# A weight subtraction on GpSimd issued as four instructions of 256 columns in place of one of 1024

## The chip, the cores and the metric

The kernel runs on one core of a Trainium2 chip. A core has five engines with an instruction queue each: TensorE (PE, with its weight loads shown apart as PEld), VectorE (DVE), ScalarE (ACT), GpSimd (POOL) and SyncE (SP, which here issues the DMAs). Engines wait for each other by semaphores. The metric is device microseconds of one execution; lower is better. The kernel before takes 1645.46 us, the median of three runs from 1644.57 to 1647.92.

## The reference

One step of a small diffusion backbone on 128 context tokens and 512 latent tokens, 1024 wide, in float32. There are two layers: layer 0 mixes tokens by a bidirectional gated linear recurrence, layer 1 by a convolution of width 31; each is followed by a squared-ReLU MLP four times as wide. Each sub-layer has this form:

```
hp = rmsnorm(xp, norm_mlp[i]) * (1.0 + m_ctx[4]) + m_ctx[3]
hs = rmsnorm(xs, norm_mlp[i]) * (1.0 + m_lat[4]) + m_lat[3]
xp = xp + m_ctx[5] * sqrelu_mlp(hp, mlp_w1[i], mlp_w2[i])
xs = xs + m_lat[5] * sqrelu_mlp(hs, mlp_w1[i], mlp_w2[i])
```

The scales, shifts and gates come from a matrix product of the conditioning vector (the modulation). Nearly all of the work is in dense products: the mixers' projections and the MLPs.

## The kernel before

Activations are kept with the model's width on the 128 partitions and the 640 tokens on the columns, in two token halves (320 and 320, later 304 and 336). A dense product is cut into units: one unit makes 128 outputs of one token half out of 1024 inputs, in eight steps k of 128 inputs.

To keep float32 accuracy, each factor is split into a high part, which the fast matmul format represents, and a low part, the rest. A step is then three matmuls: high weights by high activations (L178), low weights by high activations (L181), high weights by low activations (L182). A unit has 24.

The weights of a unit come by one DMA of 128 x 1024 into `rw` (4 buffers). ACT casts them to `wh` (L161, 5 buffers), and then POOL or DVE subtracts: `wl = rw - wh` (L163, 5 buffers). Which of the two does it is fixed by the unit's place in the list of weights (L162): POOL takes units 0 and 2, the 32 of the output projection (listed once per token half) and of layer 0's first MLP quarter, every second one of the next 48, and then 144 in a row up to the middle of layer 1's MLP; DVE takes the others, most of the first 40 and the last 70 among them. POOL does 202, DVE 132. The function `fetch` (L154) is called so that the weights of a unit are requested three units ahead of its matmuls.

DVE and ACT also do what follows a product: `hr` and the splits `ch`/`cl`, `dh`/`dl` of the MLP's hidden activations (L167, L168, L701, L702), the residual additions `xr` (L285), the squares and sums of a norm (`nsq` on ACT L254, `nacc` on DVE L255), the normed and modulated values `nt` (L276, L268) with their splits, the taps of the convolution `ps_cv` (L792) with its layer norm (`lsum` L804, `yc` L820), and the dot products of the modulation (`scratch`, L128). Such steps are put between the units by a budget per unit (`between`, L193). A scheduler beneath writes each engine's queue in the order in which the program issues, with waits where a tile is read or overwritten.

Of the kernel before, what the change touches and what calls it, by code (L numbers as in the profile page):

```python
# [9 lines left out]
F32 = mybir.dt.float32  # L10
# [3 lines left out]
ALU = mybir.AluOpType  # L14
# [3 lines left out]
D = 1024  # L18
KT = D // P
# [50 lines left out]
def hybrid_step(ctx: ExitStack, tc: tile.TileContext, xt, vec, pos, masks, ident_in, state, c_rows, w_mod0, w_modt,  # L70
# [23 lines left out]
    def v(name):  # L94
        return vt[:, VEC[name]]

# [1 line left out]
    mod = const.tile([P, 2, 48, 2], F32, name="mod")  # L98
    amod = const.tile([P, 2, 2, KT, 2], F32, name="amod")

    def mod_done(layer, j, src):
        """Adds the bias to chunks 2j and 2j+1, and for a chunk that scales makes norm_w * (1 + scale)."""
        bm = ap(vt, VEC["b_mod"].start + layer * 48 + j * 16, [[4, 4], [1, 4], [0, 2]])
        dst = ap(mod, (layer * 48 + j * 16) * 2, [[8, 4], [2, 4], [1, 2]])
        dve.tensor_tensor(dst, src, bm, ALU.add)
        for which in range(2):
            if j != (0, 2)[which]:
                continue
            base = (layer * 48 + (8, 32)[which]) * 2
            nw = VEC[("norm_mix", "norm_mlp")[which]].start + layer * 8  # L110
            dve.scalar_tensor_tensor(
                amod[:, layer, which].rearrange("p k s -> p (k s)"), ap(mod, base, [[1, 16]]), 1.0,
                ap(vt, nw, [[1, 8], [0, 2]]), ALU.add, ALU.mult)

    def mod_steps(cbs, raw_m, scratch, layer, j0, wm):
        """Chunks from 2 * j0 on of a layer's modulation, as dot products along rows of the transposed weights."""
        for s in range(2):
            cr = raw.tile([P, D], F32, tag="rw", name="cr")
            sync.dma_start(cr[:], c_rows[s:s + 1].partition_broadcast(P))
            act.activation(cbs[:, s], cr[:], AF.Sigmoid)  # L120
            dve.tensor_tensor(cbs[:, s], cbs[:, s], cr[:], ALU.mult)
        box = {}

        def step(i, s):
            if s == 0:
                box["w"] = wm()
                sync.dma_start(box["w"][:], w_modt[layer * 32 + i - 16 * (1 - layer)])
            tc.keep_in_program_order(dve.scalar_tensor_tensor(  # L128
                scratch, box["w"][:], 1.0, cbs[:, s], ALU.mult, ALU.mult, accum_out=raw_m[:, i, s:s + 1]))
            if s == 1 and i % 16 == 15:  # L130
                mod_done(layer, i // 16, ap(raw_m, (i - 15) * 2, [[8, 4], [2, 4], [1, 2]]))

        return [lambda i=i, q=q: step(i, q) for i in range(16 * j0, 48) for q in range(2)]
# [1 line left out]
    def mvec(layer, chunk, m, s):  # L135
        return mod[:, layer, chunk * 8 + m, s:s + 1]

# [1 line left out]
    MLP = [[[w_mlp[l, c, u] for u in range(16)] for c in range(4)] for l in range(2)]  # L139
    PW1 = [w_pw1[u] for u in range(16)]  # L140
    PW2 = [w_pw2[u] for u in range(8)]
# [12 lines left out]
    def fetch(upto):  # L154
        while len(split_w) < min(upto, len(plan)):
            i = len(split_w)
            rw = raw.tile([P, KT, P], F32, tag="rw", name="rw")
            sync.dma_start(rw[:], plan[i])
            wh = wpool.tile([P, KT, P], F32R, tag="wh", name="wh")
            wl = wpool.tile([P, KT, P], F32R, tag="wl", name="wl")  # L160
            act.copy(wh[:], rw[:])  # L161
            eng = pool if i in (0, 2) or 40 <= i < both_n or busy <= i < calm or (both_n <= i < busy and i % 2) else dve  # L162
            eng.tensor_tensor(wl[:], rw[:], wh[:].bitcast(F32), ALU.subtract)  # L163
            split_w.append((wh, wl))

    def split(src, hi, lo, eng=dve):
# [39 lines left out]
            bg.pop(0)[1]()  # L206

    def linear(n, acts, evac, cols, group=8, after=between, u0=0, done=None):
        """n units of weights against the token halves given in cols: {half: (lo, hi)}."""
        first = pos_w[0]  # L210
        pos_w[0] += n
        for g0 in range(0, n, group):
            us = range(g0, min(g0 + group, n))
            for half in cols:
                lo, hi = cols[half]
                for u in us:
                    fetch(first + u + 3)
                    evac(u0 + u, half, lo, hi, half_unit(split_w[first + u], acts[half], hi - lo))
                    after()
                if done and g0 + group >= n:  # L220
                    done(half)

# [1 line left out]
    def inv_rms(tp, acc, n, by_token):  # L224
        """1/rms of the columns of acc, the squares summed along D but for the partitions, on all partitions."""
        ps = axp.tile([P, 512], F32, tag="ax", name="ps_n")
        if not by_token:
            pe.matmul(ps[:, :n], ones[:], acc, start=True, stop=True)
# [10 lines left out]
        for i in range(4):  # L239
            pe.matmul(ps[:, i * c:(i + 1) * c], rc[:c, i:i + 1].broadcast_to([c, P]), ident[:c, :c],  # L240
                      start=True, stop=True)
        return ps[:, :n]

    def rms_stat(tp, xs, n, by_token=False):
        """Steps that leave 1/rms over the KT tiles xs(k) in the returned box."""
        box = {}

        def sq(k):
# [49 lines left out]

    both = {0: COLS[0][0], 1: COLS[0][1]}

# [1 line left out]
    h = {0: new_act("a"), 1: new_act("b")}  # L302
    first_ps = [[(mmp, "mm"), (scp, "sc")][half][0].tile([P, 512], F32, tag=("mm", "sc")[half], name=f"ps_f{half}")
                for half in (0, 1) for _ in range(3)]
    with tc.tile_pool(name="start", bufs=1) as st:
# [24 lines left out]
                act.activation(t[:], x0[:, k], AF.Square)  # L330
                dve.tensor_tensor(acc[k // 4][:], acc[k // 4][:], t[:], ALU.add)

        # shift and scale in blocks of columns, so that the first products start with the first block
        wmb = {}

        def first_load(m0, m1):
# [79 lines left out]
                {"L": first_load, "M": first_mods, "N": first_norm, "P": first_vecs}[a[0]](*BLOCKS[i])  # L416
        pos_w[0] = 3
        sync.dma_start(vt[:, n0:], vec[:, n0:])
        # forget gate lower bounds: softmax over the layer axis, cumulated, less the first row
        lbt = const.tile([P, 16], F32, name="lbt")  # L420
        lbe = const.tile([P, 16], F32, name="lbe")
        lbr = const.tile([P, 16], F32, name="lbr")
# [38 lines left out]
    with tc.tile_pool(name="wm0", bufs=1) as wmp, tc.tile_pool(name="hd", bufs=1) as hd:  # L461
# [31 lines left out]
            return evac  # L493

        def blocks(x, y, evac, w=SB, other=False):
            """Scores within blocks of w tokens (or across two neighbours), source token on the partition."""
            ps = scp.tile([P, 512], F32, tag="sc", name="ps_sc")
            for t in range(NTILE):
                for r in range(0, P, w):
# [4 lines left out]
            evac(ps[:, :NTILE * w].rearrange("p (t c) -> p t c", c=w))  # L504

        def decay(hs, li):
            """Keeps the operands of a level aside and takes the running products one level up."""
            lv = LEVELS[li]
            a = hs.a
            nb = NT // (2 * lv)  # L510
# [30 lines left out]
            decay(hs, 0)  # L541

        def score(hs, li):
            """li < 0: equal tokens; else the pairs that part at that level."""
            if li < 0:
                hs.sc = hd.tile([P, NTILE, SB], F32, tag="scs", name="scs")
                blocks(hs.ks[:], hs.q[:], lambda ps: act.copy(hs.sc[:], ps))
# [105 lines left out]
        while todo or mods:  # L653
            (todo or mods).pop(0)()

# [1 line left out]
    xpool = ctx.enter_context(tc.tile_pool(name="xpool", bufs=1))  # L657
    xr = xpool.tile([P, KT, NT], F32, name="xr")
    tp = ctx.enter_context(tc.tile_pool(name="tp", bufs=1))
# [33 lines left out]
    oright.close()  # L693
    rp = ctx.enter_context(tc.tile_pool(name="rp", bufs=2))

# [1 line left out]
    def hid_evac(hid):  # L697
        def evac(u, half, lo, hi, ps):
            n = hi - lo
# [15 lines left out]
        linear(8, hid, residual(xr, layer, 5), cols, group, done=done)  # L715

    def start_norm(layer, which, half, cols, first=True, by_token=False, on_dve=ND):
        """Queues a norm of one token half; returns its last step."""
        h[half] = new_act("ab"[half])
        steps = norm_steps(tp, xr, layer, which, h[half], *cols, by_token, on_dve)  # L720
        bg[:] = steps + bg if first else bg + steps
# [3 lines left out]
    A1, B1 = ({0: COLS[1][0]}, {1: COLS[1][1]})  # L725
    both1 = {0: COLS[1][0], 1: COLS[1][1]}

    # w_out, then the first MLP; the first token half runs ahead of the second
    budget[1] = 3.0
    for cols in (A0, B0):  # L730
        linear(8, on, residual(xr, 0, 2), cols, done=lambda half: start_norm(0, 1, half, COLS[0][half], False, TM0, ND0))
# [235 lines left out]
```

## Time and profile before

| what | before |
|---|---|
| timed runs | 1644.57, 1645.46, 1647.92 us |
| profiled execution: span, first to last instruction | 1641.7 us |
| PE busy | 1586.2 us, 97% |
| DVE busy | 1315.9 us, 80% |
| ACT busy | 765.8 us, 47% |
| POOL busy | 530.0 us, 32% |
| POOL's 202 subtractions wl | 504.2 us, 2502 ns each |
| mean granted clock of TensorE | 0.984 |

The page gives the profiled execution's span and no time of its own around it. Busy time is the union of an engine's instructions; a wait is idle time of an engine right before an instruction, put down to what ended it. The span is one execution with profiling, the timed runs are others without.

### The profile page before, as it was taken

Reading aid. Unit: us, or ns where it says so; the run is one execution under the profiler, and the core shown is the slowest. Engines: PE = TensorE matmul, PEld = TensorE weight load, DVE = VectorE, ACT = ScalarE, POOL = GpSimd, SP = SyncE. Lnnn points to the kernel's source line nnn. Section 1 sums busy time; section 2 is a strip of 40 time slices with the busy share of each in tenths; the row PEclk is TensorE's granted clock in tenths of the full one; section 3 lists DMA queues with packets and bytes.
Section 4 is the critical chain, followed back from the end, with each engine's and each line's share of the span. In section 5 each row is a group of like instructions: output and inputs, shape, how many; then the busy total and the mean of one; then the engine's idle time right before and its main releaser. Section 6 shows DMA issues by size and latency. Waiting matters only on the chain.

```text
span 1641.7 us, 31432 instructions
## 1 busy us (share of the span) xinstructions
PE 1586.2 (97%) x12810; PEld 1542.8 (94%) x12810; DVE 1315.9 (80%) x2222; ACT 765.8 (47%) x1227; POOL 530.0 (32%) x257
## 2 busy tenths in 40 slices
PE   8999999999998999999999999999999899999997
PEld 7899999988898999999999999989999899999997
DVE  5788888878778998888989998999999767555544
ACT  3666655566355314334443435664344545334331
POOL 3100000002363423333666665567776520000000
PEclk8999999999998999999999999999999999999999
DMA  9333333334243566676444443334444344444411
GB/s 364 117 111 118 116 110 113 120 95 158 99 148 107 173 205 219 220 227 207 155 130 153 144 152 130 124 126 162 154 154 155 100 158 154 142 141 142 142 39 65
DMA packets 71296, 240.06 MB, mean 146 GB/s; under 512 B 7792, under 2 KB 14576, under 8 KB 70128
## 3 DMA queue, kind: packets, MB, share of 16 engines
q1 hardware_dynamic: 71152, 238.06, 43.7%
q8 instruction: 101, 1.65, 0.4%
q14 instruction: 43, 0.35, 0.1%
HBM read 234.36 MB, written 3.67 MB: 145 GB/s over the span
## 4 chain that ended last, share of the span: by engine, by line
PE 61%; DVE 29%; ACT 4%; issue 3%; POOL 2%; DMA 1%; SPq 0%; DVEq 0%; ACTq 0%; POOLq 0%
PE ps_mm L178 18%; PE ps_mm L182 18%; PE ps_mm L181 18%; DVE ps_cv L792 6%; DVE cl L168 3%; DVE scratch L128 3%; DVE nacc L255 2%; POOL wl L163 2%; DVE hr L702 2%; PE ps_sc L502 2%; DVE dl L168 1%; DVE wl L163 1%; DVE nt L276 1%; DVE nt L268 1%; ACT wh L161 1%
## 5 line engine op out<-in xcount | busy, mean ns | idle before, releaser
L163 POOL TENSOR_TENSOR wl<-rw,wh 128x1024 fp32r<-128x1024 f32 x202 | 504.2, 2502 | 754.7 <-ACT wh L161 705.2
L161 ACT CAST wh<-rw 128x1024 fp32r<-128x1024 f32 x334 | 348.4, 1046 | 314.5 <-PE ps_mm L182 220.8
L178 PE MATMUL ps_mm<-bh,wh 128*128 128x320 f32 (+1 forms) x1000 | 317.7, 318 | 2.9 <-DVE ub L770 1.6
L178 PE MATMUL ps_mm<-ah,wh 128*128 128x320 f32 (+1 forms) x1000 | 314.8, 315 | 4.6 <-DVE hr L702 2.7
L182 PE MATMUL ps_mm<-al,wh 128*128 128x320 f32 (+1 forms) x1000 | 310.8, 311 | 2.6 <-DVE al L168 2.6
L181 PE MATMUL ps_mm<-bh,wl 128*128 128x320 f32 (+1 forms) x1000 | 311.2, 311 | 0.0
L181 PE MATMUL ps_mm<-ah,wl 128*128 128x320 f32 (+1 forms) x1000 | 311.1, 311 | 0.0
L182 PE MATMUL ps_mm<-bl,wh 128*128 128x320 f32 (+1 forms) x1000 | 310.8, 311 | 0.0
L792 DVE SCALAR_TENSOR_TENSOR ps_cv<-ub,vt,ps_cv 128x319 f32<-128x319 f32 (+1 forms) x464 | 228.5, 553 | 0.4
L178 PEld LDWEIGHTS ps_mm<-ah,wh 128*128 128x128 f32 x1000 | 191.4, 191 | 9.8 <-issue 3.1
L182 PEld LDWEIGHTS ps_mm<-al,wh 128*128 128x128 f32 x1000 | 191.2, 191 | 4.0 <-DVE al L168 3.1
L181 PEld LDWEIGHTS ps_mm<-ah,wl 128*128 128x128 f32 x1000 | 191.4, 191 | 3.2 <-issue 2.6
L178 PEld LDWEIGHTS ps_mm<-bh,wh 128*128 128x128 f32 x1000 | 188.0, 188 | 5.8 <-DVE ub L770 1.9
L163 DVE TENSOR_TENSOR wl<-rw,wh 128x1024 fp32r<-128x1024 f32 x132 | 162.5, 1232 | 38.7 <-ACT wh L161 38.7
L181 PEld LDWEIGHTS ps_mm<-bh,wl 128*128 128x128 f32 x1000 | 187.9, 188 | 0.5
L182 PEld LDWEIGHTS ps_mm<-bl,wh 128*128 128x128 f32 x1000 | 188.1, 188 | 0.1
L182 PE MATMUL ps_mm<-dl,wh 128*128 128x320 f32 (+1 forms) x576 | 180.7, 314 | 2.4 <-DVE dl L168 2.4
L182 PE MATMUL ps_mm<-cl,wh 128*128 128x320 f32 (+1 forms) x576 | 177.5, 308 | 5.0 <-DVE cl L168 5.0
L178 PE MATMUL ps_mm<-dh,wh 128*128 128x320 f32 (+1 forms) x576 | 181.6, 315 | 0.0
L181 PE MATMUL ps_mm<-dh,wl 128*128 128x320 f32 (+1 forms) x576 | 180.2, 313 | 0.0
L178 PE MATMUL ps_mm<-ch,wh 128*128 128x320 f32 (+1 forms) x576 | 177.9, 309 | 0.4 <-ACT ch L167 0.4
L285 DVE SCALAR_TENSOR_TENSOR xr<-ps_mm,mod,xr 128x128 f32<-128x128 f32 (+2 forms) x240 | 97.4, 432 | 99.8 <-PE ps_mm L182 99.8
(209 smaller groups left out, 2625.4 us busy)
## 6 DMA issues: line engine op xcount, KB each, us to landing
rw<-in_w_mlp SPq DMA_DIRECT2D x230, 512.0 KB, 3.3
wm<-in_w_modt SPq DMA_DIRECT2D x80, 512.0 KB, 4.1
rw<-in_w_pw SPq DMA_DIRECT2D x48, 512.0 KB, 3.3
rw<-in_w_in SPq DMA_DIRECT2D x40, 512.0 KB, 3.5
wmb<-in_w_mod SPq DMA_DIRECT2D x8, 1024.0 KB, 10.1
rw<-in_w_out SPq DMA_DIRECT2D x16, 512.0 KB, 3.4
x<-in_xt SPq DMA_DIRECT2D x8, 320.0 KB, 5.5
xr<-in_xt SPq DMA_DIRECT2D x8, 320.0 KB, 5.8
```

Of the source, the lines that this page charges most:

```text
L128: tc.keep_in_program_order(dve.scalar_tensor_tensor(scratch, box["w"][:], 1.0, cbs[:, s], ALU.mult, ALU.mult, accum_out=raw_m[:, i, s:s + 1]))
L161: act.copy(wh[:], rw[:])
L163: eng.tensor_tensor(wl[:], rw[:], wh[:].bitcast(F32), ALU.subtract)
L168: eng.tensor_tensor(lo, src, hi.bitcast(F32), ALU.subtract)
L178: first = pe.matmul(ps[:, :n], wh[:, k, :], hi[:, :n], start=k == 0, stop=False)
L181: pe.matmul(ps[:, :n], wl[:, k, :], hi[:, :n], start=False, stop=False)
L182: pe.matmul(ps[:, :n], wh[:, k, :], lo[:, :n], start=False, stop=k == KT - 1)
L255: dve.tensor_tensor(box["acc"][:, :n], box["acc"][:, :n], t[:, :n], ALU.add)
L285: dve.scalar_tensor_tensor(x[:, u, a:b], ps[:, a - lo:b - lo], mvec(layer, chunk, u, s), x[:, u, a:b], ALU.mult, ALU.add)
L502: pe.matmul(ps[r:r + w, t * w:(t + 1) * w], x[:, s0:s0 + w], y[:, t0:t0 + w], start=True, stop=True, tile_position=(0, r))
L702: dve.tensor_tensor(r[:, :n], ps, r[:, :n], ALU.mult)
L792: dve.scalar_tensor_tensor(box[i][:, :m], u[:, j:j + m], w, box[i][:, :m], ALU.mult, ALU.add)
```

## The change

The subtraction of L163 is put into a loop. On POOL it is issued four times, each over two of the eight steps k, that is 256 of 1024 columns; on DVE the loop has one turn and the instruction is as before. Comments are taken out, which moves line numbers (the subtraction is L165 after, the matmuls L180, L183 and L184).

```diff
             eng = pool if i in (0, 2) or 40 <= i < both_n or ... else dve
-            eng.tensor_tensor(wl[:], rw[:], wh[:].bitcast(F32), ALU.subtract)
+            step = KT // 4 if eng is pool else KT
+            for k in range(0, KT, step):
+                eng.tensor_tensor(wl[:, k:k + step], rw[:, k:k + step], wh[:, k:k + step].bitcast(F32), ALU.subtract)
             split_w.append((wh, wl))
```

POOL's queue from the start to the first MLP, before (`x` counts equal instructions in a row; `bl` are low activations, `xr` the residual stream):

```order
L163 TENSOR_TENSOR wl<-rw,wh 128x1024 x2
L168 TENSOR_TENSOR bl<-x_129,bh 128x320 x4
L433 CAST mask<-mf 128x160
L168 TENSOR_TENSOR bl<-x_129,bh 128x320 x4
L441 MEMSET sel 128x64
L442 MEMSET sel 128x1
L163 TENSOR_TENSOR wl<-rw,wh 128x1024
L297 TENSOR_TENSOR xr<-xr,pe_t 128x512 x8
L163 TENSOR_TENSOR wl<-rw,wh 128x1024 x59
```

And the same piece of POOL's queue after:

```order
L165 TENSOR_TENSOR wl<-rw,wh 128x256 x8
L170 TENSOR_TENSOR bl<-x_129,bh 128x320 x4
L435 CAST mask<-mf 128x160
L170 TENSOR_TENSOR bl<-x_129,bh 128x320 x4
L443 MEMSET sel 128x64
L444 MEMSET sel 128x1
L165 TENSOR_TENSOR wl<-rw,wh 128x256 x4
L299 TENSOR_TENSOR xr<-xr,pe_t 128x512 x8
L165 TENSOR_TENSOR wl<-rw,wh 128x256 x236
```

Each subtraction has become four in its own place, and nothing else has moved. PE's queue at the start of the first unit of the output projection (`ch`, `cl` are activations), with the semaphores that each matmul waits for, before:

```order
L181 MATMUL ps_mm<-ch,wl 128x320 [waits Pool_49]
L182 MATMUL ps_mm<-cl,wh 128x320
L178 MATMUL ps_mm<-ch,wh 128x320 [waits Activation_49]
L181 MATMUL ps_mm<-ch,wl 128x320
L182 MATMUL ps_mm<-cl,wh 128x320
L178 MATMUL ps_mm<-ch,wh 128x320 [waits Activation_49]
L181 MATMUL ps_mm<-ch,wl 128x320
L182 MATMUL ps_mm<-cl,wh 128x320
```

And after:

```order
L183 MATMUL ps_mm<-ch,wl 128x320 [waits Pool_49]
L184 MATMUL ps_mm<-cl,wh 128x320
L180 MATMUL ps_mm<-ch,wh 128x320 [waits Activation_49]
L183 MATMUL ps_mm<-ch,wl 128x320
L184 MATMUL ps_mm<-cl,wh 128x320
L180 MATMUL ps_mm<-ch,wh 128x320 [waits Activation_49]
L183 MATMUL ps_mm<-ch,wl 128x320 [waits Pool_49]
L184 MATMUL ps_mm<-cl,wh 128x320
```

PE's order is the same; the matmul with low weights waits for POOL once in two steps k instead of once a unit. The orders on DVE, ACT and SP are the same before and after.

## Rows read from the trace of the kernel before

**Rows 1.** The page's busy time of each engine: us, share of span, instructions.

```profile
PE 1586.2 (97%) x12810; PEld 1542.8 (94%) x12810; DVE 1315.9 (80%) x2222; ACT 765.8 (47%) x1227; POOL 530.0 (32%) x257
```

**Rows 2.** Windows: stretch, length, busy us (instructions) by engine, clock, DMA.

```profile
480.00:1340.00 860.00, 823.22 (x5536) 814.79 (x5535) 771.90 (x1332) 383.64 (x600) 463.82 (x209) 0.98 0.49 160
780.00:830.00 50.00, 45.49 (x294) 44.50 (x293) 47.47 (x67) 24.13 (x43) 28.74 (x27) 0.97 0.44 148
1110.00:1290.00 180.00, 170.97 (x1189) 168.80 (x1188) 174.01 (x347) 79.02 (x115) 122.90 (x52) 0.98 0.45 150
```

**Rows 3.** Waits of PE, 480 to 1340: us in total, times, longest us.

```profile
PE ps_n L228 <- DVE nacc L255: 8.8, 4, 3.2
PE ps_n L236 <- DVE nacc L255: 7.6, 1, 7.6
```

**Rows 4.** Costliest groups: busy us, mean ns | idle us ahead, what ended most.

```profile
L163 POOL TENSOR_TENSOR wl<-rw,wh 128x1024 fp32r<-128x1024 f32 x202 | 504.2, 2502 | 754.7 <-ACT wh L161 705.2
...
L181 PE MATMUL ps_mm<-ah,wl 128*128 128x320 f32 (+1 forms) x1000 | 311.1, 311 | 0.0
```

**Rows 5.** Instructions of nacc and scratch on DVE: ns min/median/max, first and last start.

```profile
L255 DVE TENSOR_TENSOR nacc<-nacc,nsq x70: 444/502/2679, 448.5 to 1631.9; 128x320 f32<-128x320 f32 x28, 128x304 f32<-128x304 f32 x21, 128x336 f32<-128x336 f32 x21
...
L128 DVE SCALAR_TENSOR_TENSOR scratch<-wm,cbs x96: 1206/1215/3299, 515.1 to 799.0; 128x1024 f32<-128x1024 f32 x96
```

**Rows 6.** Timeline of POOL and DVE near 1043: start us, length us, instruction.

```profile
1042.81 2.40 POOL L163 TENSOR_TENSOR wl<-rw,wh 128x1024 fp32r<-128x1024 f32 x1 [8.54 <-ACT wh L161]
...
1045.17 2.65 POOL L163 TENSOR_TENSOR wl<-rw,wh 128x1024 fp32r<-128x1024 f32 x1
...
1043.14 2.42 DVE L255 TENSOR_TENSOR nacc<-nacc,nsq 128x320 f32<-128x320 f32 x1 [0.34 <-ACT nsq L254]
...
1043.14 7.59 DVE L255 TENSOR_TENSOR nacc<-nacc,nsq 128x320 f32<-128x320 f32 x3 [0.34 <-ACT nsq L254]
```

**Rows 7.** Timeline of POOL and DVE near 58, two POOL subtractions of 320 columns.

```profile
57.91 0.88 POOL L168 TENSOR_TENSOR bl<-x,bh 128x320 fp32r<-128x320 f32 x1 [5.72 <-ACT bh L167]
...
58.74 1.12 POOL L168 TENSOR_TENSOR bl<-x,bh 128x320 fp32r<-128x320 f32 x1
...
58.17 0.96 DVE L168 TENSOR_TENSOR al<-x,ah 128x320 fp32r<-128x320 f32 x1
```

**Rows 8.** Timeline of POOL, six subtractions in a row from 1111.

```profile
1111.02 14.22 POOL L163 TENSOR_TENSOR wl<-rw,wh 128x1024 fp32r<-128x1024 f32 x6 [5.18 <-ACT wh L161]
```

**Rows 9.** Timeline of DVE ahead of PE's five largest stalls: the long instructions.

```profile
502.18 2.62 DVE L255 TENSOR_TENSOR nacc<-nacc,nsq 128x320 f32<-128x320 f32 x1
...
505.80 1.56 DVE L255 TENSOR_TENSOR nacc<-nacc,nsq 128x320 f32<-128x320 f32 x1 [0.54 <-ACT nsq L254]
...
540.12 3.02 DVE L128 SCALAR_TENSOR_TENSOR scratch<-wm,cbs 128x1024 f32<-128x1024 f32 x1
...
543.07 2.65 DVE L168 TENSOR_TENSOR dl<-hr,dh 128x320 fp32r<-128x320 f32 x1
...
819.25 2.26 DVE L268 TENSOR_SCALAR nt<-nt,amod,mod 128x128 f32<-128x128 f32 x1
...
823.73 2.63 DVE L276 TENSOR_TENSOR nt<-xr,rs 128x320 f32<-128x320 f32 x1
...
1266.05 2.05 DVE L804 TENSOR_TENSOR lsum<-lsum,yc 128x336 f32<-128x336 f32 x1
...
1271.86 3.54 DVE L820 TENSOR_TENSOR yc<-yc,mu 128x336 f32<-128x336 f32 x3
...
1277.76 2.84 DVE L255 TENSOR_TENSOR nacc<-nacc,nsq 128x336 f32<-128x336 f32 x2
...
1283.44 3.00 DVE L255 TENSOR_TENSOR nacc<-nacc,nsq 128x336 f32<-128x336 f32 x2 [0.28 <-ACT nsq L254]
```

**Rows 10.** Windows behind two of the stalls; the last but two column is the clock.

```profile
507.40:512.50 5.10, 5.09 (x23) 5.09 (x24) 0.65 (x2) 0.70 (x2) 0.00 (x0) 0.50 0.30 103
...
547.30:553.40 6.10, 6.08 (x23) 6.08 (x24) 5.13 (x10) 2.04 (x5) 0.00 (x0) 0.50 0.45 163
```

## The prediction

> **What bounds the kernel now.** I read the busy shares first: TensorE (PE) is busy 97% of 1641.7 us [rows 1], so only three things can move the time: PE's idle time, a lower clock, or new PE work. POOL, the engine that is edited, is busy 32%. Next the windows: of 860 us between 480 and 1340, where nearly all of POOL's subtractions run, PE is busy 823.2, so it idles 36.8 us [rows 2]; that is what a change on POOL can give back or add to. The waits name who ends that idle time: VectorE (DVE), above all its sums of squares, 7.6 us in one wait and 8.8 in four [rows 3]. No row of PE's waits there names POOL, and the groups of instructions agree: PE's products with the low weights (L181) have idle time 0.0, while POOL stands idle 754.7 us ahead of its 202 subtractions, 705.2 of it for ScalarE's casts [rows 4]. The low halves are early; making their first quarter earlier still is worth nothing to PE.
>
> So why would POOL matter? Look at one and the same DVE instruction: the sum nacc takes 0.444 us at least, 0.502 in the median, 2.679 at most, and scratch 1.206, 1.215 and 3.299 [rows 5]. The stretch of nacc around 1043 us shows why. POOL runs 1042.81 to 1045.21; nacc starts at 1043.14 and ends at 1045.56, 0.35 us after POOL did, three times in a row, 7.59 us for three [rows 6]. An addition with both operands in SBUF is held until the subtraction that runs on POOL is over. The reader is to see a second thing in these rows: POOL's second subtraction starts at 1045.17, queued right behind the first, and yet nacc gets in between them; the subtraction takes 2.65 instead of 2.40. A waiting DVE instruction gets through after one POOL instruction, and costs POOL 0.25.
>
> **The change part by part.** Removed: 202 POOL subtractions of 1024 columns. Added: 808 of 256 columns. Everything else stands in the same order on every engine; PE gets three more waits on POOL for each of 202 units.
>
> Price of a piece. Two POOL subtractions of 320 columns stand back to back, the second starting 58.74 - 57.91 = 0.83 us after the first [rows 7]; six of 1024 columns take 14.22 us, 2.37 each [rows 8]. The line through both is 0.13 + 0.00219 per column: 0.69 for 256 columns, 2.76 for four, 0.39 more per unit, 79 us over 202. Bounds: a piece can't be under a quarter of 2.37 (0.59, if nothing is fixed) nor over the 0.83 that 320 columns took; four cost 2.37 to 3.32. I take 0.69, nearest to the 320 columns in size. The cover is POOL's idle time, and what is queued behind POOL's pieces are its own next pieces and a few memsets. Between 1110 and 1290 POOL is busy 122.9 of 180 us in 52 instructions [rows 2]; with 0.39 on each that is 143, still inside. Cover gone is a rival below.
>
> The Perfetto Trace Analysis page of the Trainium skill (section GPSIMD Engine Instruction) advises to time POOL by start-to-start spacing, not by reported durations. By durations (0.88 for 320 columns, 2.40 for 1024 [rows 6, 7]) the line would give 0.74 a piece and 2.96 for four; the sum below would lose another 2 us.
>
> Added waits on PE: 606 more, each on a piece that is long done. L181's idle time of 0.0 with 202 such waits today [rows 4] prices them at 0; if one cost the 0.02 us of a semaphore instruction that I allow as the upper end, 606 cost 12.
>
> Shorter holds on DVE. A DVE instruction that arrives at random in a POOL instruction waits half of it: 1.18 us now, 0.35 with pieces. POOL is running 2.76/2.37 = 1.17 times as long, so 0.35 of the waiting stays and 0.65 goes. Rows 7 show the pattern at nearly the new size: the DVE subtraction al, caught in a 320-column POOL piece, took 0.96, not 2.4, and the next piece 1.12 instead of 0.88. I count the DVE rows ahead of PE's five largest stalls [rows 9], with 0.5 as the free length (rows 5) of an instruction of about 320 columns, and 1.21 for scratch:
> - 500 to 507: two nacc, 2.62 and 1.56, so 3.2 held; 0.65 of it 2.1. The wait is 7.6 [rows 3], so much of it stays.
> - 540 to 547: scratch 3.02 and dl 2.65, 4.0 held, 2.6 back.
> - 818 to 827: nt 2.26 and nt 2.63, 3.9 held, 2.5 back.
> - 1043 to 1050: three nacc in 7.59, 6.1 held, 4.0 back, but the wait is only 3.2 [rows 3]: 3.2.
> - 1266 to 1287: lsum 2.05, three yc in 3.54, two nacc in 2.84, two in 3.00: 1.5 + 2.0 + 1.8 + 2.0 = 7.4 held, 4.8 back.
>
> Together 15.2. The five places can't take more than 7.6 + 4.0 + 3.9 + 3.2 + 7.4 = 26 of the 36.8 us; the other 10.5 lie in short waits where one DVE instruction in between is late, of which I take 4. What is late next: the casts on ScalarE between two DVE steps of a norm, and PE itself.
>
> Room for both. Between 780 and 830 DVE is busy 47.5 of 50 us and POOL 28.7 [rows 2]: there the two already exclude each other most of the time, and POOL's extra time must come from somewhere. 27 POOL instructions less 16 memsets are 11 subtractions, 11 x 0.39 = 4.3 us; I charge all of it.
>
> Clock. Right after a long stall the granted clock is 0.50, its lower level of 1.2 GHz: 23 matmuls in 5.1 us after 507, 23 in 6.1 after 547 [rows 10], against 860/5536 = 0.155 each over the stretch with its stalls: 1.5 and 2.5 us lost. The stall at 544 should all but vanish and take its stretch along, that of 507 shrink; with the shorter ones behind other stalls I take 3.
>
> Sum: 15.2 + 4 - 4.3 + 3 = 17.9 us less. The profiled execution's span goes from 1641.7 to 1623.8. The three timed runs lie 2.9 to 6.2 us above that span, the median 3.8, time around the span that the edit doesn't touch; 1645.5 - 18 = 1627.5.
>
> **The rivals.**
> - POOL falls behind (slower). Place: 800 to 1330, where every unit's low half is POOL's and PE takes 24 matmuls of 171/1189 = 0.144, 3.45 us, a unit. A piece at its upper bound, 0.83, makes 3.32; with one DVE instruction let in, 0.25, 3.57 a unit. From 0.80 a piece on, POOL is the slower one and the spare buffers only delay it. Some 150 units (530 us by 3.45) late by 0.12 each are 18 us; DVE, held by a POOL that never rests, gets back only half of the forecast's gain, 9: 18 - 9, 9 us slower, 1654. For it: each piece offers another place for a DVE instruction to push in. Against: the 0.83 was measured for 320 columns, a fourth more.
> - POOL's four queued pieces don't let DVE in between. Then a hold is 2.76 instead of 2.37, the waits of 36.8 us grow by 0.17: 6 us slower, 1651.5. The GPSIMD Engine Reference of the Trainium skill (section Instruction dispatch) speaks for it: each of POOL's eight cores starts the next instruction as soon as its own share of the last is done, without waiting for the others, so there need be no moment at which all have let go. Against: in rows 6 and 7 the second POOL instruction was queued and ready, and DVE got in each time.
> - No change: DVE's holds shrink but PE's stalls are ended by something beside them (the casts, the order of the queue), as most of the 7.6 us are: 15.2 + 4 falls to a quarter, 5, less 4.3: 1645.
> - More than forecast: all holds at the five places (22, by each wait's limit) and half of the 10.5 vanish and the clock never falls there (6): 33 us, 1612.
> - PE's added waits are not free: 12 us of them eat most of the gain: 1639.5.
>
> **How the numbers follow.** A difference below 0.2%, 3.3 us, can't be told from none here. Forecast (10 to 26 us less) 0.52; more 0.12; added waits or a half-behind POOL (4 to 10 less) 0.12; no change 0.08; POOL behind 0.10; DVE not let in 0.06. Faster 0.76, same 0.08, slower 0.16. The likeliest case's own range is 1619.5 to 1635.5; for 8 in 10, with the bounds 0.59 and 0.83, I go from 1612 to 1650.
>
> **What would show it.** POOL: 808 subtractions, start to start near 0.69, busy time near 580 to 620 us. The longest nacc, cl and dl near 1.2 instead of 2.6; scratch near 2 instead of 3.3. PE's waits for DVE between 480 and 1340 near 20 us, the stall at 544 gone, that at 500 still there. L181 still without idle time. I am wrong if nacc still takes 2.4 us beside POOL (not let in), if PE waits for wl (POOL behind), or if DVE's holds shrink and PE's stalls stay (no change).

## The result, and the profile after

The changed kernel takes 1619.37 us (median of four runs, 1616.84 to 1620.54), beside it the kernel before 1646.66 (four runs): ratio 0.9837, 95% interval 0.9823 to 0.9851. That is 27.3 us less; 1627.5, 18 less, was forecast.

The profiled execution's span falls from 1641.7 to 1614.9 us. The page of the changed kernel, its busy times as in [rows 1]:

```profile
PE 1578.3 (98%) x12810; PEld 1536.0 (95%) x12810; DVE 1249.4 (77%) x2222; ACT 761.9 (47%) x1227; POOL 694.0 (43%) x863
```

The 26.8 us split in two. Span less PE's busy time is PE's idle time: 55.5 before, 36.6 after, 18.9 less. The other 7.9 are PE's busy time itself, for the same 12810 matmuls: the mean granted clock is 0.989 instead of 0.984. A second profile of the changed kernel (below) splits its gain into 16.6 and 7.4. DVE, whose instructions are the same 2222, is busy 66.5 us less. The time in which it was held counted as its busy time.

The windows of the changed kernel, to be laid beside [rows 2]; the second row is the stretch between the two matmuls that the kernel before starts at 780 and 830 us, so it holds the same work as the second row there. The first columns are length, PE, PEld, DVE, ACT and POOL, the last but two the granted clock:

```profile
480.00:1320.00 840.00, 821.40 (x5609) 815.02 (x5608) 725.85 (x1341) 384.92 (x611) 617.64 (x767) 1.00 0.50 166
773.04:820.96 47.92, 45.17 (x294) 44.22 (x293) 40.25 (x67) 24.30 (x43) 41.34 (x61) 0.96 0.47 154
```

PE's idle time in the stretch of POOL's work goes from 36.8 to 18.6 us. The second row is the place with "no room for both": POOL is now busy 41.3 us instead of 28.7, and still DVE needs only 40.3 us, instead of 47.5, for the same 67 instructions, and the stretch is 2.1 us shorter.

PE's waits in the changed kernel between 470 and 1320 (in total, times, longest, in us), where [rows 3] were:

```profile
PE ps_n L230 <- DVE nacc L257: 2.8, 2, 1.7
PE ps_n L238 <- DVE nacc L257: 2.6, 1, 2.6
PE ps_mm L180 <- ACT nt L268: 2.6, 1, 2.6
PE ps_mm L180 <- ACT ch L169: 2.3, 1, 2.3
PE ps_mm L180 <- DVE xr L287: 2.1, 2, 1.3
PE ps_mm L184 <- DVE cl L170: 1.8, 5, 0.9
```

The 7.6 for nacc has become 2.6 and the 8.8 has become 2.8; waits for ScalarE, the next in the chain, have moved up. The groups that answer to [rows 4], from the page:

```profile
L165 POOL TENSOR_TENSOR wl<-rw,wh 128x256 fp32r<-128x256 f32 x808 | 668.8, 861 | 568.1 <-ACT wh L161 561.6
...
L183 PE MATMUL ps_mm<-ah,wl 128*128 128x320 f32 (+1 forms) x1000 | 308.0, 308 | 0.0
```

The added waits of PE cost nothing: 0.0 again. Last the tiles that DVE makes, as in [rows 5] (ns, minimum, median, maximum):

```profile
L257 DVE TENSOR_TENSOR nacc<-nacc,nsq x70: 444/527/7968, 451.3 to 1604.2; 128x320 f32<-128x320 f32 x28, 128x304 f32<-128x304 f32 x21, 128x336 f32<-128x336 f32 x21
L128 DVE SCALAR_TENSOR_TENSOR scratch<-wm,cbs x96: 1208/1236/1768, 512.0 to 789.6; 128x1024 f32<-128x1024 f32 x96
L170 DVE TENSOR_TENSOR dl<-hr,dh x64: 493/502/1043, 529.4 to 1548.9; 128x320 fp32r<-128x320 f32 x32, 128x336 fp32r<-128x336 f32 x32
```

The holds are as long as a piece now: dl 1.04, scratch 1.77. One row doesn't fit: a nacc of 7.97 us. The timeline near 1040, on POOL and then on DVE, shows the common case (start and length in us, xN equal instructions in a row):

```profile
1039.58 5.28 POOL L165 TENSOR_TENSOR wl<-rw,wh 128x256 fp32r<-128x256 f32 x6
...
1041.52 1.02 DVE L257 TENSOR_TENSOR nacc<-nacc,nsq 128x304 f32<-128x304 f32 x1
1042.46 0.86 DVE L270 TENSOR_SCALAR nt<-nt,amod,mod 128x320 f32<-128x320 f32 x1
1043.24 1.01 DVE L257 TENSOR_TENSOR nacc<-nacc,nsq 128x304 f32<-128x304 f32 x1
```

Six pieces take 5.28, 0.88 each, because a DVE instruction gets in after each. And near 1291, POOL and DVE, stands the row that doesn't fit:

```profile
1287.43 11.18 POOL L165 TENSOR_TENSOR wl<-rw,wh 128x256 fp32r<-128x256 f32 x16
...
1291.00 7.97 DVE L257 TENSOR_TENSOR nacc<-nacc,nsq 128x336 f32<-128x336 f32 x1 [1.03 <-ACT nsq L256]
```

Here sixteen pieces run 0.70 apart without a break, to 1298.60, where POOL's work in the kernel ends. Only then, at 1298.97, is nacc done. It was shut out for eleven pieces, the one that ran when it came among them.

### The profile page after: what moved, and what is told of

The parts are those of the page before. It is cut to its first block, busy times and chain, and to the rows that moved or that the text cites. A ratio compares the mean times of both kernels' runs of the same rounds, so it can differ in the third digit from the quotient of the medians.

```text
span 1614.9 us, 32111 instructions
## 1 busy us (share of the span) xinstructions
PE 1578.3 (98%) x12810; PEld 1536.0 (95%) x12810; DVE 1249.4 (77%) x2222; ACT 761.9 (47%) x1227; POOL 694.0 (43%) x863
## 4 chain that ended last, share of the span: by engine, by line
PE 76%; DVE 17%; POOL 2%; ACT 2%; issue 2%; DMA 0%; SPq 0%; DVEq 0%; POOLq 0%; ACTq 0%
PE ps_mm L180 23%; PE ps_mm L184 22%; PE ps_mm L183 22%; DVE ps_cv L794 3%; POOL wl L165 2%; DVE scratch L128 2%; PE ps_sc L504 2%; DVE nt L278 1%; DVE nacc L257 1%; DVE cl L170 1%; PE ps_u L588 1%; DVE hr L704 1%; DVE nt L270 1%; DVE yc L822 1%; DVE al L170 1%
## 5 line engine op out<-in xcount | busy, mean ns | idle before, releaser
L165 POOL TENSOR_TENSOR wl<-rw,wh 128x256 fp32r<-128x256 f32 x808 | 668.8, 861 | 568.1 <-ACT wh L161 561.6
L180 PE MATMUL ps_mm<-bh,wh 128*128 128x320 f32 (+1 forms) x1000 | 317.8, 318 | 2.8 <-ACT nt L268 2.6
L180 PE MATMUL ps_mm<-ah,wh 128*128 128x320 f32 (+1 forms) x1000 | 311.6, 312 | 1.9 <-ACT ah L169 1.1
L183 PE MATMUL ps_mm<-bh,wl 128*128 128x320 f32 (+1 forms) x1000 | 311.4, 312 | 0.0
L184 PE MATMUL ps_mm<-bl,wh 128*128 128x320 f32 (+1 forms) x1000 | 310.8, 311 | 0.0
L184 PE MATMUL ps_mm<-al,wh 128*128 128x320 f32 (+1 forms) x1000 | 308.0, 308 | 1.7 <-DVE al L170 1.7
L183 PE MATMUL ps_mm<-ah,wl 128*128 128x320 f32 (+1 forms) x1000 | 308.0, 308 | 0.0
L165 DVE TENSOR_TENSOR wl<-rw,wh 128x1024 fp32r<-128x1024 f32 x132 | 168.7, 1280 | 39.6 <-ACT wh L161 39.6
L180 PEld LDWEIGHTS ps_mm<-ah,wh 128*128 128x128 f32 x1000 | 188.6, 189 | 7.3 <-issue 3.4
L180 PEld LDWEIGHTS ps_mm<-bh,wh 128*128 128x128 f32 x1000 | 188.0, 188 | 5.7 <-ACT nt L268 2.8
L183 PEld LDWEIGHTS ps_mm<-ah,wl 128*128 128x128 f32 x1000 | 188.5, 188 | 3.2 <-issue 2.6
L184 PEld LDWEIGHTS ps_mm<-al,wh 128*128 128x128 f32 x1000 | 188.6, 189 | 3.1 <-DVE al L170 2.2
L183 PEld LDWEIGHTS ps_mm<-bh,wl 128*128 128x128 f32 x1000 | 187.9, 188 | 0.5
L184 PEld LDWEIGHTS ps_mm<-bl,wh 128*128 128x128 f32 x1000 | 188.1, 188 | 0.1
L180 PE MATMUL ps_mm<-ch,wh 128*128 128x320 f32 (+1 forms) x576 | 176.8, 307 | 4.4 <-ACT ch L169 2.3
L180 PE MATMUL ps_mm<-dh,wh 128*128 128x320 f32 (+1 forms) x576 | 180.7, 314 | 0.0
L184 PE MATMUL ps_mm<-dl,wh 128*128 128x320 f32 (+1 forms) x576 | 180.0, 313 | 0.0
L183 PE MATMUL ps_mm<-dh,wl 128*128 128x320 f32 (+1 forms) x576 | 179.7, 312 | 0.0
L184 PE MATMUL ps_mm<-cl,wh 128*128 128x320 f32 (+1 forms) x576 | 176.7, 307 | 1.8 <-DVE cl L170 1.8
```

The lines of the kernel that those rows point to most:

```text
L165: eng.tensor_tensor(wl[:, k:k + step], rw[:, k:k + step], wh[:, k:k + step].bitcast(F32), ALU.subtract)
L180: first = pe.matmul(ps[:, :n], wh[:, k, :], hi[:, :n], start=k == 0, stop=False)
L183: pe.matmul(ps[:, :n], wl[:, k, :], hi[:, :n], start=False, stop=False)
L184: pe.matmul(ps[:, :n], wh[:, k, :], lo[:, :n], start=False, stop=k == KT - 1)
```

## The experiments

The theory: the gain is shorter holds of DVE by POOL. Rivals: PE gains because the first quarter of a low half is there sooner; or only the number of instructions counts. All times stand beside runs of the kernel before on the same chip (medians 1643.8, 1644.7 and 1645.1 for the first four, the next four and the last three); "idle" is span less PE's busy time of the profiled execution.

| version | us, median (range) | ratio (95%) | span | PE busy | idle |
|---|---|---|---|---|---|
| two pieces | 1623.37 (1621.53 to 1626.76) | 0.9877 (0.9855 to 0.9899) | 1624.9 | 1582.5 | 42.4 |
| eight pieces | 1648.45 (1641.77 to 1651.81) | 1.0019 (1.0002 to 1.0036) | 1646.1 | 1589.6 | 56.5 |
| four, last to first | 1618.75 (1616.82 to 1620.55) | 0.9843 (0.9822 to 0.9863) | 1618.7 | 1582.0 | 36.7 |
| four, late units only | 1627.34 (1626.05 to 1629.24) | 0.9900 (0.9882 to 0.9918) | 1625.4 | 1579.7 | 45.7 |
| four, units 0 and 2 whole | 1618.50 (1615.75 to 1621.01) | 0.9840 (0.9818 to 0.9862) | 1619.1 | 1582.1 | 37.0 |
| four, early units only | 1634.77 (1630.92 to 1636.60) | 0.9932 (0.9906 to 0.9959) | 1634.0 | 1586.4 | 47.6 |
| the same as the fifth, two at the end | 1618.49 (1617.10 to 1619.48) | 0.9840 (0.9821 to 0.9859) | 1617.2 | 1580.0 | 37.2 |
| eight pieces and a memset | 1648.46 (1644.48 to 1653.70) | 1.0019 (1.0002 to 1.0036) | 1642.3 | 1588.5 | 53.8 |
| the changed kernel again | 1620.03 (1614.10 to 1620.76) | 0.9844 (0.9825 to 0.9862) | 1617.7 | 1578.8 | 38.9 |
| three pieces | 1619.64 (1619.45 to 1622.05) | 0.9852 (0.9839 to 0.9866) | 1619.6 | 1580.0 | 39.6 |
| four, and two at two places | 1615.81 (1614.81 to 1617.03) | 0.9826 (0.9813 to 0.9840) | 1614.1 | 1577.2 | 36.9 |

**Two pieces.**

```diff
-            step = KT // 4 if eng is pool else KT
+            step = KT // 2 if eng is pool else KT
```

> Two pieces of 512 columns instead of four of 256. Theory (a POOL instruction holds a DVE instruction with two SBUF operands until it ends, so the length of one POOL instruction sets the wait): the longest nacc falls from 2.68 us to about 1.6 (1.24 of a piece and 0.35), a piece steps 1.24 to 1.27, and the gain is between those of one and four pieces: 0.45 of the waiting goes instead of 0.65, so 16 to 22 us under the kernel before. Rival (what helps is that the first low weights are ready earlier): with half of a subtraction instead of a quarter ready at the first semaphore, most of the gain stays too, 20 us or more; this run alone doesn't tell the two apart, it gives the second point of the curve. Rival (added waits on PE cost, and four pieces had three more each): two pieces do better than four.

Measured 20.4 us less, and the two rows of wl on POOL and nacc on DVE in this kernel are:

```profile
L165 POOL TENSOR_TENSOR wl<-rw,wh x404: 1262/1297/2386, 21.6 to 1306.4; 128x512 fp32r<-128x512 f32 x135
L257 DVE TENSOR_TENSOR nacc<-nacc,nsq x70: 444/507/1574, 450.3 to 1615.1; 128x320 f32<-128x320 f32 x28, 128x304 f32<-128x304 f32 x21, 128x336 f32<-128x336 f32 x21
```

The longest nacc has the length of a piece and a little, and no DVE instruction with two operands in SBUF waited for more than the piece that ran. Halving the hold brings most of the gain, and with holds of 2.68, 1.57 and 1.03 the times fall in that order.

**Eight pieces.**

```diff
-            step = KT // 4 if eng is pool else KT
+            step = KT // 8 if eng is pool else KT
```

> Eight pieces of 128 columns. A piece should step 0.42 us (line through 0.70 for 256 columns and 2.36 for 1024), eight take 3.4, against about 3.45 us that PE needs for a unit in the stretch 800 to 1290; with DVE instructions let in at up to eight places, POOL is the slower engine there. Theory of the hold, with its limit: the longest nacc falls to about 0.8, but PE now waits for wl and the gain is mostly or wholly lost, between 10 us under and 20 us over the kernel before. Rival of the early first piece: finer is better, at least as fast as four pieces (1619). A subtraction done late would show in PE's waits for wl, of which there are none so far.

The whole gain is gone, as the theory's limit had it, but by another way: not by waits for wl. PE's waits in this kernel between 470 and 1330, the two longest groups:

```profile
PE ps_mm L180 <- DVE xr L287: 12.5, 5, 5.4
PE ps_mm L180 <- DVE hr L704: 6.2, 3, 5.7
```

PE waits for DVE in single waits of 5 us, and never for a low half wl. What makes DVE late shows at 1052, on POOL and on DVE:

```profile
1049.66 10.47 POOL L165 TENSOR_TENSOR wl<-rw,wh 128x128 fp32r<-128x128 f32 x25
1063.14 1.12 POOL L165 TENSOR_TENSOR wl<-rw,wh 128x128 fp32r<-128x128 f32 x2 [3.01 <-ACT wh L161]
...
1051.83 0.56 DVE L287 SCALAR_TENSOR_TENSOR xr<-ps_mm,mod,xr 128x128 f32<-128x128 f32 x2
1052.30 8.58 DVE L278 TENSOR_TENSOR nt<-xr,rs 128x320 f32<-128x320 f32 x2
```

25 pieces run 0.42 apart until POOL has none that is ready (it then waits 3.01 for a cast), and nt ends 0.35 after the last: 8.18 of the 8.58 are the first of the two. There are six such rows of 5.0 to 9.9 us, at 863, 884, 1052, 1086, 1142 and 1184. Between the matmuls that the kernel before starts at 865 and 902 us PE loses 11.0 here, where the changed kernel gains 1.2. Not all of the loss is of this kind: between the matmuls that the kernel before starts at 560 and 600 us PE loses 7.5 (2.7 in the changed kernel) though no row shuts DVE out there. DVE stands idle there for the modulation's weights, and the residual additions queued behind that instruction come late:

```profile
583.11 1.49 DVE L128 SCALAR_TENSOR_TENSOR scratch<-wm,cbs 128x1024 f32<-128x1024 f32 x1 [7.65 <-DMA wm<-in_w_modt]
```

**Four pieces, the last columns first.** PE's first need is the piece that comes last, so that PE waits for all of a low half.

```diff
-            for k in range(0, KT, step):
+            for k in reversed(range(0, KT, step)):
```

> Four pieces, issued from the last columns to the first, so that PE's first product with the low weights waits for the whole subtraction as it did before the change, and the three later waits are long satisfied. Theory of the hold: as fast as four pieces in order, 1616 to 1623. Rival (the early first quarter is what helps): the gain is gone, 1640 to 1652.

The ratio is that of the change, and so is PE's idle time, 36.7. PE gains nothing from a piece that is early.

**Four pieces for the late units only, and for the early units only.**

```diff
-            step = KT // 4 if eng is pool else KT
+            step = KT // 4 if eng is pool and i >= busy else KT    # late: 144 units
+            step = KT // 4 if eng is pool and i < busy else KT     # early: 58 units
```

> Four pieces only for the 144 units in a row from the second token half of layer 0's MLP on; the first 58 of POOL's subtractions stay whole. By PE's lead over the kernel before at the same matmul (6.0 us at 583 us, of which the start had lost 3.2, and 26.9 at the end), the late part is worth 18 to 21 us: 1625 to 1629, with the stalls of PE at 500 and 544 us back as before (7.6 and 2.7 us) and the stalls after 800 as short as with four pieces everywhere. If the gain came from one place or from the clock of the start alone, this run shows 0 or the whole 27.

> Four pieces for the units before the 144 of the second half (58 units), whole subtractions for the 144. The late pieces alone gained 16.4 us, all pieces 24.4 by the same base. If the places add up, the early ones alone gain 8.0: 1635.8, with the stall at 544 gone, the one at 1043 still there with nacc near 2.5, and 7.5 at the longest PE wait for nacc down to about 2.6. Rival: a place that is made earlier only hands its time to a later wait (then the parts gain more alone than together): 12 us or more, 1632.

Late alone gains 16.4, early alone 10.0 us, 26.4 together, against 24.4 to 27.3 for all. With the late ones alone the wait of 7.6 at nacc and one of 2.7 for hr at 544 stay, with the early ones alone nacc at 1043 still ends a wait of 3.2, as in [rows 3], and the wait of 7.6 is 2.6. By the times alone both readings of the expectation stay open, as the interval of the early version is 6.7 to 15.5 us. The traces decide: PE's lead over the kernel before at the same matmul is 6.6 at 583 us with the early pieces alone and still 7.8 at the end. The places add up; what the early place gains isn't taken back by waits of the other half.

**Units 0 and 2 whole, then also two pieces for POOL's last 8 units.**

```diff
-            step = KT // 4 if eng is pool else KT
+            step = KT // 4 if eng is pool and i > 2 else KT
+            step = (KT if i <= 2 else KT // 2 if i >= calm - 8 else KT // 4) if eng is pool else KT
```

> Units 0 and 2 are subtracted whole, as before; all other units of POOL in four pieces. In the changed kernel PE was 3.2 us later than before at 43 us, with a half-clock stretch at 32 us that the kernel before has not. If the pieces at the start cause that (POOL's additional time for units 0 and 2 delays its own low activations bl behind them), the stretch is gone, PE is back level at 43 us, and the time is 1616. Rival: the start varies with other things (the version with late pieces alone, whose start is that of before, was 1.0 us late there): the stretch stays and the time is 1619.5, that of the changed kernel.

> As the version before it (units 0 and 2 whole), and POOL's last 8 units in two pieces of 512 instead of four. In the changed kernel, and in two others with four pieces, a nacc at POOL's last 11 pieces took 7.97 us and got in only when POOL had no piece left. If a row of short pieces is what shuts it out, it takes under 1.7 us here, and PE gets up to the 2.6 us of its wait behind it: 1613.5 to 1616. Rival: the shutting out goes with the place and not with the length of the pieces: the nacc near 1290 is again held until POOL's end, over 5 us, and the time is that of the version before it or slower.

The start was a misreading. Windows of 25 to 45 us in the changed kernel, its second profile, and the two versions with whole units 0 and 2 (last but two: the clock):

```profile
25.00:45.00 20.00, 17.71 (x103) 13.43 (x104) 13.07 (x24) 3.35 (x9) 7.92 (x9) 0.74 0.80 321
```

```profile
25.00:45.00 20.00, 17.25 (x113) 12.81 (x117) 14.35 (x25) 3.52 (x9) 9.25 (x9) 0.84 0.79 317
```

```profile
25.00:45.00 20.00, 17.95 (x104) 13.60 (x105) 12.68 (x24) 3.42 (x9) 5.81 (x5) 0.74 0.80 318
```

```profile
25.00:45.00 20.00, 17.76 (x130) 13.34 (x130) 14.53 (x25) 5.33 (x12) 6.96 (x6) 0.95 0.79 314
```

One and the same start has 0.74 and 0.95, and pieces have 0.74 and 0.84. The clock of the start scatters between executions by some 4 us of time, whatever the pieces: at 43 us PE is 3.2, 2.0 and 3.1 behind the kernel before in the first three, and 1.1 ahead in the fourth. At the end nacc is no longer shut out, as the theory had it: its longest in the kernel is 1.32 us. But the time is the same, and between the matmuls that the kernel before starts at 1256 and 1293 us PE gains 4.2, where it gained 4.3 with nacc shut out. So that shut-out cost nothing that can be measured; the 2.6 us that I had set on it were wrong. What kept nacc out isn't settled by this run either: with two pieces the row is shorter in pieces as well as made of longer ones (last section).

**Eight pieces and a memset.** Is it the kind of instruction that keeps the door shut?

```diff
+    gap = const.tile([P, 1], F32, name="gap")
-            step = KT // 4 if eng is pool else KT
+            step = KT // 8 if eng is pool else KT
+                if k == KT // 2 and eng is pool:
+                    tc.keep_in_program_order(pool.memset(gap[:], 0.0))
```

> Eight pieces of 128 columns with a memset of one column on POOL between the fourth and the fifth, about 0.1 us a unit. With eight pieces alone DVE instructions were shut out for 12 to 23 pieces, 5.0 to 9.9 us, six times, and the time was 1648.5. If another kind of instruction on POOL, which reads nothing, opens the door, no DVE instruction passes more than 8 pieces, 3.6 us, and most of the gain comes back: 1625 to 1635. Rival: only a POOL without a ready instruction opens it: rows of 12 pieces and more again, 5 us or more, and 1648 to 1656.

The rival holds. This kernel's DVE and POOL near 1177:

```profile
1176.98 11.76 DVE L809 TENSOR_TENSOR lsum<-lsum,yc 128x336 f32<-128x336 f32 x1
...
1176.91 3.38 POOL L168 TENSOR_TENSOR wl<-rw,wh 128x128 fp32r<-128x128 f32 x8
1180.24 0.09 POOL L167 MEMSET gap<- 128x1 f32 x1
1180.30 3.38 POOL L168 TENSOR_TENSOR wl<-rw,wh 128x128 fp32r<-128x128 f32 x8
1183.63 0.09 POOL L167 MEMSET gap<- 128x1 f32 x1
1183.68 3.36 POOL L168 TENSOR_TENSOR wl<-rw,wh 128x128 fp32r<-128x128 f32 x8
```

Three memsets of 0.09 pass, and lsum stays outside for 27 pieces. But not even the rival is all of it: lsum is done at 1188.7, and POOL's row goes on without a pause, with its next memset at 1190.9.

**The changed kernel again, three pieces, and four with two at two places.** The last has two pieces for ten units near 1040 us, where nt is shut out, and for POOL's last eight.

```diff
-            step = KT // 4 if eng is pool else KT
+            step = 3 if eng is pool else KT    # with slices cut at KT: 384, 384, 256
+            step = (KT // 2 if busy + 66 <= i < busy + 76 or i >= calm - 8 else KT // 4) if eng is pool else KT
```

> The changed kernel once more, beside the next two. Its median was 1619.4; 1617 to 1620.5 expected. Its first trace had one long shut-out, of nacc at 1291, and three siblings with the same four pieces at that place had a second one, of nt near 1040 (5.5 us). If chance decides, this trace may have it or not; where it has, PE should lose about 2.7 us more between 1050 and 1070. At the start PE stood 3.2 us behind the kernel before in the first trace, and 3.1 behind and 1.1 ahead in two siblings whose start is issued alike: somewhere in -3 to +1 here.

> Three pieces a unit, of 384, 384 and 256 columns. By the line through the measured steps a piece of 384 takes 0.97 and a unit 2.64. If only the length of a hold counts, the gain lies between that of two pieces (20) and that of four (24): 1621. If the seldom shut-outs of short pieces eat what shorter holds would give, three pieces beat four: 1616 to 1618, with no DVE instruction passing three pieces or more.

> Four pieces, but two for the 10 units that POOL splits around 1040 us and for its last 8 units. If the shut-out of nt near 1040 costs PE some 2.7 us, and two pieces can't bring it about, nt takes at most 1.6 there, PE loses under 3.5 between 1050 and 1070 instead of 5.6, and the time is about 1616. Rival: the shut-outs only move to another place, or PE's loss there is made up later: 1618.5 to 1620.

The second profile of the changed kernel has the shut-out that the first lacks, POOL and DVE near 1040:

```profile
1035.45 9.06 POOL L165 TENSOR_TENSOR wl<-rw,wh 128x256 fp32r<-128x256 f32 x13
...
1039.51 5.75 DVE L278 TENSOR_TENSOR nt<-xr,rs 128x320 f32<-128x320 f32 x2
```

So the same program has it in one execution and not in another. Between the matmuls that the kernel before starts at 1062 and 1081 us PE loses 5.65 here against 2.90 in the first profile: 2.75 us is the shut-out's price in that stretch, as expected. With two pieces there the same two instructions are held by no more than a piece:

```profile
1036.99 2.37 DVE L278 TENSOR_TENSOR nt<-xr,rs 128x320 f32<-128x320 f32 x2
```

PE loses 3.66 there (under 3.5 was expected). At 1615.81 this is the fastest version, 4.2 below the changed kernel beside it; the intervals, 0.9813 to 0.9840 and 0.9825 to 0.9862, overlap, so the trace shows the mechanism and the times alone don't prove the gain. Of the 3.6 us between the two profiled spans this stretch has 2.0, and 2.3 come from the start, whose clock scatters. Three pieces have no shut-out at all and take 1619.64, the same as four. That would fit longer holds and fewer shut-outs in balance, but no run separates the two.

## Why the prediction was right, and where its sizes were off

The direction, the mechanism and the stated range (1612 to 1650) held. The size was 27 instead of 18, just past the likeliest case's own range of 10 to 26, to which I had given 0.52, and short of "more than forecast", 33, to which I had given 0.12. PE's matmuls can be matched by number, 12810 in either trace. The difference of their starts, read at the ends of a stretch (us of the kernel before), is what PE gained there. Less PE's waits it is the busy time that PE saved on the same matmuls, put down to the clock (read up to the start of the last matmul, 0.1 more than the difference of the spans):

| stretch | what | forecast, without the clock | measured | of it idle time | of it busy time |
|---|---|---|---|---|---|
| 0 to 43 | start | 0 | -3.2 | 0.4 | -3.6 |
| 402 to 515 | stall at 500 | 2.1 | 5.9 | 5.0 | 0.8 |
| 515 to 556 | stall at 544 | 2.6 | 5.7 | 2.7 | 3.0 |
| 556 to 583 | two new waits, xr and hr | 0 | -2.7 | -2.1 | -0.7 |
| 796 to 830 | stalls at 818 to 827 | 2.5 | 2.1 | 1.8 | 0.3 |
| 1032 to 1062 | stall at 1047 | 3.2 | 5.1 | 3.2 | 1.9 |
| 1062 to 1081 | new wait for nt | 0 | -2.9 | -2.4 | -0.5 |
| 1256 to 1293 | stalls at 1266 to 1284 | 4.8 | 5.2 | 2.2 | 3.0 |
| the rest | short waits 4, no room -4.3 | -0.3 | 11.7 | 8.0 | 3.8 |
| together | | 14.9 and 3 for the clock | 26.9 | 18.8 | 8.1 |

The 9 us that the forecast fell short are 4 of idle time and 5 of the clock.

- **Five stalls.** They gave back 14.9 of idle time, against 15.2. In sum this step was right, but with some luck, as two places are off by about as much in opposite ways: 5.0 instead of 2.1 at 500, 2.2 instead of 4.8 at 1266 to 1284. "What is late next" was named and put at nothing; it took 4.5. It came true in part: the new wait at 1054 ends on ScalarE, though on nt and not on a cast; those at 566 and 574 end on DVE's hr and xr. At 500 I counted two nacc of [rows 9]; in the trace after they take 1.02 and 0.62 instead of 2.62 and 1.56, 2.5 less instead of 2.1; the al ahead of them, which I hadn't counted, takes 0.49 instead of 1.34. That is 3.4 of the 5.0 by which PE's wait is shorter (7.6 to 2.6); the rest isn't split further.
- **Short waits and room, a step that failed.** I took 4 for the short waits and charged 4.3 for POOL's extra time between 780 and 830; idle time in the rest of the kernel fell by 8.0, of it 2.7 between 830 and 1032 and 4.4 between 1081 and 1256. The charge hardly shows: between 780 and 830 PE gained 2.1, where 2.5 less 4.3 was forecast. It rested on DVE's 47.5 busy us of 50 [rows 2], and part of these were holds: with shorter ones DVE needs 40.3 for the same instructions and leaves POOL its room. A busy share of an engine that is held isn't all work, and can't be added to another's.
- **Clock, the term that was mis-sized most.** 8 instead of 3, and that with 3.6 lost at the start, where the clock scatters; between 402 and 1293 it gave 12. I read two stretches at half clock [rows 10]; between 500 and 1300 there were seven, also behind the short stalls. The other five and the whole of the first, in the kernel before:

```profile
502.30:512.50 10.20, 5.09 (x23) 5.09 (x24) 5.18 (x5) 2.45 (x4) 4.71 (x2) 0.50 0.57 206
...
823.10:826.50 3.40, 3.40 (x15) 3.40 (x14) 3.36 (x4) 2.05 (x5) 2.38 (x1) 0.50 0.32 127
1024.50:1027.90 3.40, 3.40 (x11) 3.06 (x12) 2.95 (x2) 3.37 (x5) 3.39 (x2) 0.50 0.05 11
1051.80:1055.20 3.40, 3.40 (x16) 3.40 (x15) 0.66 (x2) 3.08 (x4) 3.40 (x2) 0.50 0.68 241
1270.30:1273.70 3.40, 3.40 (x15) 3.40 (x14) 2.75 (x5) 3.14 (x7) 1.26 (x1) 0.50 0.05 20
1287.30:1290.70 3.40, 3.40 (x16) 3.40 (x15) 2.19 (x3) 1.59 (x2) 1.03 (x1) 0.51 0.24 93
```

  and, in the changed kernel, its two stretches at half clock between 500 and 1300, and three windows at full clock around the work of the stretches at 1024, 1051 and 1270:

```profile
506.60:510.00 3.40, 3.40 (x16) 3.40 (x15) 0.49 (x1) 0.90 (x2) 3.16 (x5) 0.50 0.90 325
813.80:817.20 3.40, 2.84 (x11) 2.84 (x12) 3.36 (x8) 2.57 (x5) 2.40 (x3) 0.50 0.49 154
1006.00:1018.00 12.00, 10.32 (x69) 9.93 (x68) 10.01 (x17) 8.58 (x14) 8.43 (x12) 1.00 0.30 96
1030.00:1040.00 10.00, 10.00 (x73) 9.84 (x72) 4.47 (x9) 5.88 (x8) 10.00 (x15) 1.00 0.46 159
...
1240.00:1252.00 12.00, 11.27 (x80) 10.84 (x79) 10.29 (x18) 6.36 (x12) 10.19 (x13) 1.00 0.39 131
```

  Two of the three windows at full clock still hold waits of PE (10.32 busy of 12, 11.27 of 12). I had read the clock only where I had read a stall.
- **Time around the span.** I took the 3.8 us between the profiled span and the median time as fixed. In the runs beside the experiments it is 1.9 to 2.3 for each execution itself; the rest was scatter between executions. The 18 us don't depend on it.
- **Price of a piece.** 0.69 was forecast, 11.18 / 16 = 0.70 measured. POOL's busy time, 694 instead of 580 to 620, is off because each DVE instruction that gets in lengthens a piece: 861 ns in the mean against a median of 741, 808 x 0.12 = 97 us. The Perfetto Trace Analysis page of the Trainium skill (section GPSIMD Engine Instruction) is right here, as it goes by start-to-start spacing: that is 0.70, and the durations are 0.74.
- **Added waits.** 0, as taken: L183 has no idle time, and pieces in reversed order changed nothing.
- **Rival "falls behind".** It named PE's wait for wl as the price. With eight pieces POOL is busy 863.5 us and no wait of PE names wl; the low halves are early enough even so. The loss came through DVE, shut out by POOL and once waiting for a DMA.
- **Rival "not let in".** Seldom true with four pieces, though the sign that I had named for it, a nacc over 2.4 us, stands in the trace once. With eight pieces it is most of the story: the three stretches with its six long rows (865 to 902, 1062 to 1081 and 1081 to 1256 us of the kernel before) lose 29.5 us, where the changed kernel gains 4.0. The rule of the GPSIMD Engine Reference in the Trainium skill (section Instruction dispatch), that POOL's cores start the next instruction each on its own, makes such rows possible; these traces show them in a few of hundreds of cases, in the same places again and again, and none tells whether that rule is their cause.
- **What would show it.** PE's waits for DVE between 480 and 1320 add up to 12.5 us (near 20 expected), the stall at 544 is gone, that at 500 shrank more than I thought.

## What to carry to other kernels

Where two engines exclude each other, the length of one instruction on the idle engine is a latency of the busy one: look for one DVE instruction with a minimum and a maximum far apart, and cut what it waits behind. Two pieces gave most of the gain, four the rest, and eight gave it all back, so measure more than one size, watch for long unbroken rows of pieces, and read the longest instruction of each tile afterwards, not its median. Half-clock stretches belong to the price of a stall, also of a short one: list them all before sizing a gain.

## What the runs showed that was not expected

DVE can be shut out by a row of short POOL instructions. I took from the traces every TENSOR_TENSOR and SCALAR_TENSOR_TENSOR on DVE with no operand in PSUM that starts while a piece of wl runs, and counted the pieces that ended before it did, the running one included. In the four traces with four pieces of every unit or of all but units 0 and 2 (both of the changed kernel, the reversed one, the one with whole units at the start) 7 of 703 that came first, after a rest of DVE or after an instruction with an operand in PSUM, were passed by 8 or 11 pieces (5.3 to 8.0 us), and none of 338 that followed straight on another instruction without one. With eight pieces, with and without the memset, it was 13 of 405 firsts, passed by 5 to 27, and none of 339 followers. With pieces of 384, 512 or 1024 columns none was passed by more than two. Where in a piece the instruction arrived made no difference that I could see.

What sets the shut-out ones apart in the same count is how long POOL's row had already run at its own spacing (0.70 or 0.42 us), with no pause and no DVE instruction that made it wait. In the six traces with four pieces in the late units (in one of them but for POOL's last eight) 14 instructions met a row that had run at least 12 pieces so, and 10 of them were shut out; of 1472 that met a shorter one, none was. With eight pieces it was 13 of 28, and none of 716. The places repeat: nacc at POOL's end in all 5 traces with four pieces there, nt near 1040 in 5 of 6. The nacc of 7.97 us above came 21 pieces into a row that had begun at 1276.31:

```profile
1276.31 22.30 POOL L165 TENSOR_TENSOR wl<-rw,wh 128x256 fp32r<-128x256 f32 x32 [6.20 <-ACT wh L161]
```

This is a pattern in the traces and not a test of it: some that met such a row got in. Nor is the length of a piece shown to matter beside the count, as a row of 12 longer pieces was met only once, with 384 columns, and that instruction got in. Why a long row shuts some out stays open. Not tried was a row of pieces with a true pause in it.
